# Softmax parts without the row sums: the high part on ScalarE, the sums by transpose and DRAM into the gates

## The chip, the cores and the metric

The kernel runs on one core of a Trainium2 chip. TensorE (PE) multiplies matrices and writes into PSUM, VectorE (DVE), ScalarE (ACT) and GpSimd (POOL) work elementwise, and SyncE (SP) issues the DMAs. Each engine runs its own instructions in order and waits for others by semaphores. The metric is the device time of one execution in microseconds (us).

## The reference

One layer over 1024 frames of 1024 features: a LayerNorm, one wide projection, two attention mixers side by side, and a LayerNorm after the sum. Cut to what matters:

```
proj = h @ w_in + b_in                       # q, k, v, z of mixer A; latents and z of mixer B; two gates
ya = A(q, k, v)                              # 8 heads of 64; own chunk of 64 and 8 before it, relative bias
yb = B(q, k, v)                              # 8 heads; chunk-causal over all keys before
    s = q . k * scale (+ bias);  p = softmax(s);  y = p @ v
ya = (ya * silu(a_z)) @ w_proj_a
yb = (yb * silu(b_z)) @ w_proj_b
out = (sigmoid(g_a) * ya + sigmoid(g_b) * yb) @ w_out
h = LN(alpha * h + out)
```

## The kernel before

All large products are made of three float32r matmuls of high and low parts (`three`, lines 166 to 169). The work has three stretches: entry, LayerNorm and values (to about 174 us), attention (174 to 746 us), and the projection of mixer B with the output product (to the end). In the attention stretch two streams are woven by `run` (line 270): attention steps and the dense chunks (`Chunk`, line 171), which make q, k, z and the gates for later. The weave goes by estimated costs written in the code.

An attention step is one tile of 128 queries of one head: `scores` (lines 684 and 781) leaves the scores in a PSUM tile `ps` of two banks of 512 columns, and DVE moves them to SBUF with the row's extreme `nm` (lines 697 and 796). `softmax` (line 805) takes exp on ACT with the row sum `su`, turns the sum into a reciprocal and a scaled reciprocal on DVE, lets POOL write the float16 high part `hi` (line 816) and DVE the low part `lo` (line 817), and SP transposes both by DMA into `pT` (line 819). `pv` (line 822) multiplies with the values three tiles later in mixer A and two in mixer B (LAG_A, LAG_B; `Steps.one`, line 847). A tile has 128 to 640 key columns in A and 128 to 1024 in B. Every fourth tile `finish_y` (line 716) takes y from PSUM, and POOL multiplies it with the gate `sz` (line 728), which `evac_silu` (line 708) made from z; `sz` has two buffers, one for each half of 512 frames, and holds two heads in its 128 partitions. The result goes to DRAM (`y_d`) and is read back (`yr`) later, or, for the last heads of B, stays in SBUF as `YB`.

The tile `p16` that holds `hi` and `lo` has three buffers in A and two in B, and the ring `st` of 512 columns has five, shared by gates, y and loads. The order in which instructions stand in each engine's queue is made at build time by a scheduler that works with its own estimate of durations (line 1155); the chip then runs each queue in order. Nearly all DMAs are issued by SP: weights (line 135), transposes, gates and y.

```python
            A.activation(s[:, :n], s[:, :n], AF.Exp, scale=-1.0, bias=nm, accum_out=su)
            V.reciprocal(rc, su)
            V.tensor_scalar(rc2, rc, 2.0 ** 14, None, op0=ALU.mult)
            G.tensor_scalar(hi, s[:, :n], rc, 2.0 ** 14, op0=ALU.mult, op1=ALU.mult)
            V.scalar_tensor_tensor(lo, s[:, :n], rc2, hi, op0=ALU.mult, op1=ALU.subtract)
            SY.dma_start(pT[:, : 2 * n // P, :], p16[:, : 2 * n], transpose=True)
```

Of the kernel before, what the change touches and what calls it, by code (L numbers as in the profile page):

```python
# [18 lines left out]
P = 128  # L19
S = 1024  # L20
# [35 lines left out]
def tile_hybrid_layer(  # L56
# [45 lines left out]
    kr_d = [dram.tile([32, S], F32, name=f"kr_d{i}") for i in range(2)]  # L102
    y_d = [dram.tile([512, S], F32, name=f"y_d{i}") for i in range(2)]
    th_d = [dram.tile([D, S], F32, name=f"th_d{i}") for i in range(2)]


    ident = consts.tile([P, P], F32, name="ident")
# [519 lines left out]
    with ExitStack() as p1:  # L627
# [24 lines left out]
        class PairA:  # L652
# [31 lines left out]
            def scores(self, e, i):  # L684
                h = 2 * self.p + e
                k0 = max(0, i - 4)
                n = (i - k0 + 1) * P
                ps = ps_sc.tile([P, 2, 512], F32, tag="sc", name=f"sa{h}_{i}")
                nb, w = (1, max(n, 256)) if n <= 512 else (2, n // 2)
                for b in range(nb):  # L690
                    ks = slice(k0 * P + b * w, k0 * P + b * w + w)
                    T.matmul(ps[:, b, :w], self.sQ[e][:, i * P : (i + 1) * P], self.sK[e][:, ks], start=True, stop=False)
                    T.matmul(ps[:, b, :w], self.sX[e][:, i * P : (i + 1) * P], self.sK[e][:, ks], start=False, stop=True)
                w = min(w, n)
                s = pools["s"].tile([P, 640], F32, tag="s", name=f"ss{h}_{i}")
                nm = sm.tile([P, 1], F32, tag="nm", name=f"nm{h}_{i}")
                V.tensor_tensor_reduce(  # L697
                    s[:, :n].rearrange("p (b w) -> p b w", b=nb),
                    ps[:, :nb, :w],
                    self.tb[e][:, 640 - n : 640].rearrange("p (b w) -> p b w", b=nb),  # L700
                    -0.125, 3e38, ALU.add, ALU.min, nm,
                )
                return s, nm, n

            def tail(self, e, half, yt, r):
                finish_z(self, 0, e, half, yt, r)
# [27 lines left out]
        class PairB:  # L734
# [46 lines left out]
            def scores(self, e, i):  # L781
                h = 2 * self.p + e
                n = (i + 1) * P
                ps = ps_sc.tile([P, 2, 512], F32, tag="sc", name=f"sb{h}_{i}")
                nb, w = (1, max(n, 256)) if n <= 512 else (2, n // 2)
                qs = slice(i * P, (i + 1) * P)
                for b in range(nb):
                    ks = slice(b * w, b * w + w)
                    T.matmul(ps[:, b, :w], self.sQ[e][:, qs], self.sK[e][:, ks], start=True, stop=False)
                    T.matmul(ps[:, b, :w], self.sX[e][:, qs], self.sK[e][:, ks], start=False, stop=False)  # L790
                    T.matmul(ps[:, b, :w], self.qr[e][:, qs], krt[:, ks], start=False, stop=True)
                w = min(w, n)
                V.memset(ps[0:64, nb - 1, w - 64 : w], NEG)
                s = pools["s"].tile([P, S], F32, tag="s", name=f"sbs{h}_{i}")
                nm = sm.tile([P, 1], F32, tag="nm", name=f"nmb{h}_{i}")
                V.tensor_scalar(  # L796
                    s[:, :n].rearrange("p (b w) -> p b w", b=nb), ps[:, :nb, :w], -B_SCALE, None,
                    op0=ALU.mult, op1=ALU.min, accum_out=nm,
                )
                return s, nm, n  # L800

            def tail(self, e, half, yt, r):
                finish_z(self, 1, e, half, yt, r)

        def softmax(pair, e, i, nm_):
            s, nm, n = pair.scores(e, i)
            su = sm.tile([P, 1], F32, tag="su", name=f"su{nm_}")
            A.activation(s[:, :n], s[:, :n], AF.Exp, scale=-1.0, bias=nm, accum_out=su)  # L808
            rc = sm.tile([P, 1], F32, tag="rc", name=f"rcp{nm_}")
            V.reciprocal(rc, su)  # L810
            rc2 = sm.tile([P, 1], F32, tag="rc2", name=f"rcs{nm_}")
            V.tensor_scalar(rc2, rc, 2.0 ** 14, None, op0=ALU.mult)
            W_ = pools["w"]
            p16 = pools["p"].tile([P, 2 * W_], F16, tag="p16", name=f"p16{nm_}")
            hi, lo = p16[:, :n], p16[:, n : 2 * n]
            G.tensor_scalar(hi, s[:, :n], rc, 2.0 ** 14, op0=ALU.mult, op1=ALU.mult)  # L816
            V.scalar_tensor_tensor(lo, s[:, :n], rc2, hi, op0=ALU.mult, op1=ALU.subtract)  # L817
            pT = pools["pt"].tile([P, 2 * W_ // P, P], F16, tag="pt", name=f"pT{nm_}")
            SY.dma_start(pT[:, : 2 * n // P, :], p16[:, : 2 * n], transpose=True)
            return pT  # L820

        def pv(pair, mixer, e, i, pT, v16):
            h = 2 * pair.p + e
# [15 lines left out]
        class Steps:  # L839
# [7 lines left out]
            def one(self):  # L847
                pair, e, i = self.seq[self.at]
                self.at += 1
                nm = f"{self.m}_{2 * pair.p + e}_{i}"  # L850
                self.q.append((pair, e, i, softmax(pair, e, i, nm)))
                if i == 6:
                    self.next_head()
                if len(self.q) > self.lag:
                    self.fin()
# [5 lines left out]

            def fin(self):
                pair, e, i, pT = self.q.pop(0)
                pv(pair, self.m, e, i, pT, V16[2 * self.m + pair.p // 2])

            def units(self, n):
# [292 lines left out]
```

## Time and profile before

| | |
|---|---|
| time, median of 3 runs | 892.89 us (891.52 to 894.52) |
| the profiled execution | 892.41 us, span 890.6 us |
| instructions | 13773 |
| mean granted TensorE clock | 0.977 |
| DMA | 124.68 MB, mean 140 GB/s |

The span runs from the first to the last instruction. Clock 1 is 2.4 GHz; a mean below 1 says that part of the stretch ran at 1.2 GHz. "A <- B" in a list of waits means that engine and line A sat idle until B was done. Times in a timeline count from the span's start.

### The profile page before, as it was taken

The numbers are of one execution on the slowest core, as the hardware profiler recorded it, in microseconds if no ns is written. First come the engines' busy times: TensorE is split into PE (matmuls) and PEld (weight loads), VectorE is DVE, ScalarE is ACT, GpSimd is POOL, SyncE is SP. The second block draws the span as 40 slices with busy tenths as digits, with TensorE's granted clock in tenths as the row PEclk, the third lists the DMA queues.
The fourth block names the chain that finished last, engine by engine and source line by source line (L and its number), as shares of the span: only waits on it lengthen the run. The fifth ranks groups of instructions, "written<-read, shape, count | busy, mean of one in ns | idle before, by whom it ended". The sixth has DMA issues, their size and how long they took to land. (4 is left out here: it accounts for less than half of the span.)

```text
span 890.6 us, 13773 instructions
## 1 busy us (share of the span) xinstructions
PE 832.0 (93%) x4760; PEld 697.9 (78%) x4760; DVE 570.3 (64%) x1267; ACT 359.0 (40%) x729; POOL 397.3 (45%) x413
## 2 busy tenths in 40 slices
PE   5999899998999896999999999999998899999996
PEld 4999798887777685778787877888777787888886
DVE  6899655577687769756655655265606584657654
ACT  4234475445455535545443444354425251422000
POOL 5547541344554445834333943253445373641100
PEclk8999899999999999899999999999999899999999
DMA  6522013376678564595665567556866879551421
GB/s 204 204 106 80 32 42 101 139 150 134 147 150 173 128 145 115 99 206 115 141 154 148 107 153 149 163 119 133 186 176 134 197 194 288 178 165 60 142 95 47
DMA packets 185365, 124.68 MB, mean 140 GB/s; under 512 B 146160, under 2 KB 149744, under 8 KB 185296
## 3 DMA queue, kind: packets, MB, share of 16 engines
q1 hardware_dynamic: 185296, 123.82, 56.0%
q8 instruction: 37, 0.61, 0.3%
q14 instruction: 32, 0.26, 0.1%
HBM read 57.98 MB, written 22.81 MB: 91 GB/s over the span
## 5 line engine op out<-in xcount | busy, mean ns | idle before, releaser
L167 PE MATMUL dn<-hT,wh_c 128*128 128x512 f32 x512 | 206.6, 404 | 5.4 <-DVE sK L643 2.3
L169 PE MATMUL dn<-hT,wl_c 128*128 128x512 f32 x512 | 203.8, 398 | 0.0
L168 PE MATMUL dn<-hT,wh_c 128*128 128x512 f32 x512 | 203.3, 397 | 0.0
L132 POOL TENSOR_TENSOR wl_c<-wr_c,wh_c 128x512 fp32r<-128x512 f32 x64 | 86.1, 1346 | 117.7 <-ACT wh_c L131 103.2
L167 PEld LDWEIGHTS dn<-hT,wh_c 128*128 128x128 f32 x512 | 97.8, 191 | 24.6 <-DVE bQ L640 2.4
L169 PEld LDWEIGHTS dn<-hT,wl_c 128*128 128x128 f32 x512 | 97.6, 191 | 20.1
L168 PEld LDWEIGHTS dn<-hT,wh_c 128*128 128x128 f32 x512 | 97.9, 191 | 18.1
L817 DVE SCALAR_TENSOR_TENSOR p<-sbs,rcs,p 128x128 f16<-128x128 f32 (+3 forms) x64 | 70.2, 1099 | 24.7 <-POOL p L816 22.9
L816 POOL TENSOR_SCALAR p<-sbs,rcp 128x128 f16<-128x128 f32 (+3 forms) x64 | 49.7, 777 | 75.0 <-DVE rcp L810 57.8
L131 ACT ACTIVATE wh_c<-wr_c 128x512 fp32r<-128x512 f32 x64 | 40.3, 630 | 84.0 <-DMA wr_c<-in_wch_dram 61.2
L817 DVE SCALAR_TENSOR_TENSOR p<-ss,rcs,p 128x640 f16<-128x640 f32 (+2 forms) x64 | 59.2, 936 | 21.0 <-POOL p L816 19.9
L808 ACT ACTIVATE sbs<-sbs,nmb 128x128 f32<-128x128 f32 (+3 forms) x64 | 49.5, 774 | 56.1 <-DVE sbs L796 49.1
L728 POOL TENSOR_TENSOR yt<-yt,sz 64x512 f32<-64x512 f32 x32 | 43.4, 1355 | 52.5 <-DVE yt L722 35.7
L816 POOL TENSOR_SCALAR p<-ss,rcp 128x640 f16<-128x640 f32 (+2 forms) x64 | 45.6, 717 | 41.5 <-DVE rcp L810 27.9
L808 ACT ACTIVATE ss<-ss,nm 128x640 f32<-128x640 f32 (+2 forms) x64 | 44.4, 694 | 46.4 <-DVE nm L697 39.3
L831 PE MATMUL y<-pT,v16b 128*128 128x128 f16 x576 | 45.4, 222 | 8.6 <-DMA pT<-p 8.4
L169 PE MATMUL ops<-wo,mixT 128*128 128x512 f32 (+1 forms) x144 | 53.1, 369 | 0.0
L168 PE MATMUL ops<-wo,mixT 128*128 128x512 f32 (+1 forms) x144 | 52.9, 369 | 0.0
L831 PEld LDWEIGHTS <-v16b 128*128 128x128 f16 x576 | 33.5, 99 | 23.8 <-issue 22.6
L831 PE MATMUL y<-pT,v16a 128*128 128x128 f16 x480 | 38.4, 223 | 14.6 <-DMA pT<-p 13.4
L167 PE MATMUL ops<-wo,mixT 128*128 128x512 f32 (+1 forms) x144 | 51.7, 369 | 0.0
L831 PEld LDWEIGHTS <-v16a 128*128 128x128 f16 x480 | 28.8, 99 | 26.2 <-issue 21.1
(247 smaller groups left out, 1891.2 us busy)
## 6 DMA issues: line engine op xcount, KB each, us to landing
wr_c<-in_wch_dram SPq DMA_DIRECT2D x64, 256.0 KB, 3.1
th_d<-g SPq DMA_DIRECT2D x32, 256.0 KB, 2.5
th<-th_d SPq DMA_DIRECT2D x32, 256.0 KB, 3.3
h_d<-xt SPq DMA_DIRECT2D x8, 512.0 KB, 2.6
sX<-sQ SPq DMA_DIRECT2D x16, 256.0 KB, 4.6
sXb<-bQ SPq DMA_DIRECT2D x16, 256.0 KB, 3.9
r<-h_d SPq DMA_DIRECT2D x8, 512.0 KB, 3.5
wor<-in_wo_dram SPq DMA_DIRECT2D x16, 256.0 KB, 2.9
```

The lines of the kernel that those rows point to most:

```text
L131: A.activation(hi, raw, AF.Copy)
L132: (eng or V).tensor_tensor(lo, raw, f(hi), op=ALU.subtract)
L167: T.matmul(ps, ah, bh, start=start, stop=False)
L168: T.matmul(ps, ah, bl, start=False, stop=False)
L169: T.matmul(ps, al, bh, start=False, stop=stop)
L728: G.tensor_tensor(yt[r, :], yt[r, :], pair.sz[half][r, :], op=ALU.mult)
L808: A.activation(s[:, :n], s[:, :n], AF.Exp, scale=-1.0, bias=nm, accum_out=su)
L816: G.tensor_scalar(hi, s[:, :n], rc, 2.0 ** 14, op0=ALU.mult, op1=ALU.mult)
L817: V.scalar_tensor_tensor(lo, s[:, :n], rc2, hi, op0=ALU.mult, op1=ALU.subtract)
L831: T.matmul(o, v16[:, k0 + k, h % 4, :], pT[:, a * nk + k, :], start=(k == 0 and a == 0), stop=(k == nk - 1 and a == 1))
```

## The change

The softmax step no longer divides by the row sum. ACT writes the high part itself, as exp times 2^14 in float16, and DVE subtracts it from exp times 2^14 for the low part. The row sums of four tiles gather in the four columns of one tile `su`. Two steps after the fourth tile (at tile 1 or 5 of the next group), `norm` transposes this 128x4 tile on TensorE into columns 384 to 511 of the second bank of the current scores' PSUM tile, DVE writes the reciprocal as four rows of 128, SP stores these in DRAM (`rc_d`) and loads them back as one row of 512 broadcast to 64 partitions into a tile of the `st` ring, and POOL multiplies the half's gate `sz` with it. For the last half of a mixer's last head, `norm` runs in `fin` ahead of `pv` with a PSUM tile of its own.

```diff
@@ -102,6 +102,7 @@
     kr_d = [dram.tile([32, S], F32, name=f"kr_d{i}") for i in range(2)]
     y_d = [dram.tile([512, S], F32, name=f"y_d{i}") for i in range(2)]
     th_d = [dram.tile([D, S], F32, name=f"th_d{i}") for i in range(2)]
+    rc_d = [dram.tile([8, S], F32, name=f"rc_d{i}") for i in range(2)]
 
 
     ident = consts.tile([P, P], F32, name="ident")
@@ -700,7 +701,7 @@
                     self.tb[e][:, 640 - n : 640].rearrange("p (b w) -> p b w", b=nb),
                     -0.125, 3e38, ALU.add, ALU.min, nm,
                 )
-                return s, nm, n
+                return s, nm, n, ps
 
             def tail(self, e, half, yt, r):
                 finish_z(self, 0, e, half, yt, r)
@@ -797,27 +798,41 @@
                     s[:, :n].rearrange("p (b w) -> p b w", b=nb), ps[:, :nb, :w], -B_SCALE, None,
                     op0=ALU.mult, op1=ALU.min, accum_out=nm,
                 )
-                return s, nm, n
+                return s, nm, n, ps
 
             def tail(self, e, half, yt, r):
                 finish_z(self, 1, e, half, yt, r)
 
         def softmax(pair, e, i, nm_):
-            s, nm, n = pair.scores(e, i)
-            su = sm.tile([P, 1], F32, tag="su", name=f"su{nm_}")
-            A.activation(s[:, :n], s[:, :n], AF.Exp, scale=-1.0, bias=nm, accum_out=su)
-            rc = sm.tile([P, 1], F32, tag="rc", name=f"rcp{nm_}")
-            V.reciprocal(rc, su)
-            rc2 = sm.tile([P, 1], F32, tag="rc2", name=f"rcs{nm_}")
-            V.tensor_scalar(rc2, rc, 2.0 ** 14, None, op0=ALU.mult)
+
+            s, nm, n, ps = pair.scores(e, i)
+            if i % 4 == 0:
+                sums[pair, e, i // 4] = sm.tile([P, 4], F32, tag="su", name=f"su{nm_}")
+            A.activation(s[:, :n], s[:, :n], AF.Exp, scale=-1.0, bias=nm, accum_out=sums[pair, e, i // 4][:, i % 4 : i % 4 + 1])
             W_ = pools["w"]
             p16 = pools["p"].tile([P, 2 * W_], F16, tag="p16", name=f"p16{nm_}")
             hi, lo = p16[:, :n], p16[:, n : 2 * n]
-            G.tensor_scalar(hi, s[:, :n], rc, 2.0 ** 14, op0=ALU.mult, op1=ALU.mult)
-            V.scalar_tensor_tensor(lo, s[:, :n], rc2, hi, op0=ALU.mult, op1=ALU.subtract)
+            A.activation(hi, s[:, :n], AF.Copy, scale=2.0 ** 14)
+            V.scalar_tensor_tensor(lo, s[:, :n], 2.0 ** 14, hi, op0=ALU.mult, op1=ALU.subtract)
             pT = pools["pt"].tile([P, 2 * W_ // P, P], F16, tag="pt", name=f"pT{nm_}")
             SY.dma_start(pT[:, : 2 * n // P, :], p16[:, : 2 * n], transpose=True)
-            return pT
+            return pT, ps
+
+        sums = {}
+
+        def norm(mixer, pair, e, half, ps):
+
+
+            nm = f"{mixer}_{2 * pair.p + e}_{half}"
+            r = slice(64 * e, 64 * e + 64)
+            T.transpose(ps, sums.pop((pair, e, half)), ident)
+            row = sm.tile([4, P], F32, tag="srow", name=f"srow{nm}", bufs=2)
+            V.reciprocal(row, ps)
+            d = rc_d[mixer][2 * pair.p + e : 2 * pair.p + e + 1, half * 512 : half * 512 + 512]
+            SY.dma_start(d.rearrange("o (a b) -> (o a) b", a=4), row)
+            rb = st.tile([P, 512], F32, tag="st", name=f"rb{nm}")
+            SY.dma_start(rb[r, :], d.broadcast_to([64, 512]))
+            G.tensor_tensor(pair.sz[half][r, :], pair.sz[half][r, :], rb[r, :], op=ALU.mult)
 
         def pv(pair, mixer, e, i, pT, v16):
             h = 2 * pair.p + e
@@ -848,7 +863,11 @@
                 pair, e, i = self.seq[self.at]
                 self.at += 1
                 nm = f"{self.m}_{2 * pair.p + e}_{i}"
-                self.q.append((pair, e, i, softmax(pair, e, i, nm)))
+                pT, ps = softmax(pair, e, i, nm)
+                self.q.append((pair, e, i, pT))
+                if i in (1, 5) and self.at > 2:
+                    past = self.seq[self.at - 3]
+                    norm(self.m, past[0], past[1], past[2] // 4, ps[0:4, 1, 384:512])
                 if i == 6:
                     self.next_head()
                 if len(self.q) > self.lag:
@@ -861,6 +880,9 @@
 
             def fin(self):
                 pair, e, i, pT = self.q.pop(0)
+                if i % 4 == 3 and (pair, e, i // 4) in sums:
+                    ps = ps_sc.tile([P, 2, 512], F32, tag="sc", name=f"sup{self.m}_{2 * pair.p + e}")
+                    norm(self.m, pair, e, i // 4, ps[0:4, 0, 0:P])
                 pv(pair, self.m, e, i, pT, V16[2 * self.m + pair.p // 2])
 
             def units(self, n):
```

## Rows read from the trace of the kernel before

**Rows 1.** The page, part 1: busy us, share of span, instructions of each engine.
```profile
PE 832.0 (93%) x4760; PEld 697.9 (78%) x4760; DVE 570.3 (64%) x1267; ACT 359.0 (40%) x729; POOL 397.3 (45%) x413
```
**Rows 2.** TensorE's waits: total, times, longest us; whole span, last row 640 to 700.
```profile
PE y L831 <- DMA pT<-p: 21.9, 19, 2.6
...
PE dn L167 <- DVE sK L643: 2.3, 2, 1.6
...
PE sa L692 <- DVE nm L697: 0.6, 2, 0.3
...
PE y L831 <- DMA pT<-p: 6.4, 3, 2.6
```
**Rows 3.** Windows: stretch, length, busy us of engines, granted clock, DMA share, GB/s.
```profile
200.00:250.00 50.00, 46.13 (x295) 38.25 (x294) 32.85 (x89) 25.03 (x53) 26.18 (x32) 0.97 0.69 148
...
350.00:400.00 50.00, 44.04 (x267) 35.69 (x268) 33.90 (x74) 25.35 (x54) 32.26 (x35) 0.93 0.72 145
650.00:700.00 50.00, 43.65 (x231) 35.86 (x230) 21.62 (x52) 19.49 (x37) 21.93 (x20) 0.90 0.72 160
```
**Rows 4.** Timeline, 296 to 312 us: start, length, instruction, idle time before it.
```profile
299.28 0.19 ACT L808 ACTIVATION_READ_ACCUMULATOR ss<-ss,nm 128x1 f32 x1
...
300.64 0.79 POOL L816 TENSOR_SCALAR p<-ss,rcp 128x640 f16<-128x640 f32 x1
...
303.27 0.89 DVE L817 SCALAR_TENSOR_TENSOR p<-ss,rcs,p 128x640 f16<-128x640 f32 x1 [0.30 <-DVE rcp L810]
...
304.22 8.47 SPq L819 DMA_TRANSPOSE pT<-p  x4
...
307.64 0.83 PE L831 MATMUL y<-pT,v16a 128*128 128x128 f16 x12 [1.65 <-DMA pT<-p]
```
**Rows 5.** Timeline of ACT, DVE, SP and PE, 660 to 698 us.
```profile
662.06 0.19 ACT L808 ACTIVATION_READ_ACCUMULATOR sbs<-sbs,nmb 128x1 f32 x1
...
663.03 0.35 DVE L817 SCALAR_TENSOR_TENSOR p<-sbs,rcs,p 128x128 f16<-128x128 f32 x1 [0.40 <-POOL p L816]
...
664.54 1.18 SPq L819 DMA_TRANSPOSE pT<-p  x1
...
668.73 0.27 PE L831 MATMUL y<-pT,v16b 128*128 128x128 f16 x2 [2.06 <-DMA pT<-p]
```
**Rows 6.** Groups by line and form: count, busy us, mean ns, idle before.
```profile
L131 ACT ACTIVATE wh_c<-wr_c 128x512 fp32r<-128x512 f32 x64 | 40.3, 630 | 84.0 <-DMA wr_c<-in_wch_dram 61.2 <-PE dn L168 21.1 <-PE sa L693 1.3
...
L810 DVE RECIPROCAL rcp<-su 128x1 f32<-128x1 f32 x128 | 20.3, 160 | 45.1 <-ACT sbs L808 29.3 <-ACT ss L808 14.4
L812 DVE TENSOR_SCALAR rcs<-rcp 128x1 f32<-128x1 f32 x128 | 19.3, 152 | 3.2
...
L349 PE MATMUL hps<-ident,xt 128*128 128x128 f32 x64 | 9.3, 290 | 7.6 <-DVE xt L342 7.6
...
L533 ACT ACTIVATE v16a<-vs_a 128x256 f16<-128x256 f32 x16 | 6.5, 412 | 2.8 <-POOL vs_a L531 2.6
```
**Rows 7.** DMA issues: count, KB each, median us from issue to landing.
```profile
y_d<-yt SPq DMA_DIRECT2D x28, 128.0 KB, 2.5
yr<-y_d SPq DMA_DIRECT2D x14, 256.0 KB, 3.4
```
**Rows 8.** Waits of ACT, then of POOL, whole span.
```profile
ACT wh_c L131 <- DMA wr_c<-in_wch_dram: 61.2, 30, 6.0
...
POOL p L816 <- DMA pT<-p: 13.6, 7, 2.7
```
**Rows 9.** Timelines of POOL, ACT, DVE and PE, around the last gate and YB.
```profile
670.43 1.27 POOL L728 TENSOR_TENSOR yt<-yt,sz 64x512 f32<-64x512 f32 x1
...
681.18 0.68 ACT L712 ACTIVATE sz<-dn,bcol 128x512 f32<-128x512 f32 x1
...
749.52 0.69 DVE L132 TENSOR_TENSOR YB<-yt,YB 64x512 fp32r<-64x512 f32 x1
...
752.46 0.39 PE L167 MATMUL pj<-YB,wh_p 128*128 128x512 f32 x1
```

## The prediction

> **What bounds the kernel now.** I read the page's first part first: TensorE is busy 832.0 of 890.6 us, DVE, ACT and POOL well under two thirds [rows 1]. So the change can win only what TensorE loses, and every TensorE instruction that it adds stands on the path that sets the end. The second view was TensorE's waits. The largest by far is matmul L831 (probabilities times V) waiting for pT: 21.9 us in 19 waits, the longest 2.6; 6.4 us of that, three waits, lie between 640 and 700 us. Next come dense matmuls waiting for a PSUM buffer that DVE has not emptied: 2.3 us behind sK, and the same once more, 1.6 us, behind bQ, of which the first stands [rows 2]. The third view was the windows over the attention stage. In four of 50 us between 200 and 700 the granted clock is clearly below 1: 0.97 twice (one of them shown), 0.93 and 0.90 of 2.4 GHz [rows 3], so part of each runs at the lower level of 1.2 GHz. Matmul time lost is 1.5 + 1.5 + 3.5 + 5.0 = 11.5 us. Before the falls TensorE idled: the three windows shown have 3.9, 6.0 and 6.4 us without matmul. The pT waits with the clock behind them thus cost about 33 us, and this is what the change can reach.
>
> The fourth view, the timeline of two late tiles, shows where lateness comes from. In the first, exp with its row sum is done at 299.47; POOL begins the high part at 300.64, DVE the low part only at 303.27, the DMA transpose is issued at 304.22, and L831 runs at 307.64 after 1.65 us of waiting [rows 4]. So 4.7 us pass between the sum and the end of the low part, of which the two conversions are 0.79 + 0.89; the rest is queueing on two engines and the reciprocal. In the second tile (128 columns) the low part is done at 663.38, but the transpose is issued at 664.54 and TensorE starts at 668.73, after 2.06 us: there the DMA is late, not the arithmetic [rows 5].
>
> **The change part by part.** The sum is made on the profiled execution, 892.41 us, which is 1.8 over its span and 0.5 under the median of 892.89.
>
> *The softmax step, 128 times.* It loses a reciprocal and a scaling on DVE (20.3 + 19.3 = 39.6 us over all) [rows 6]. The high part moves from POOL (0.79 us at 640 columns, rows 4) to ACT. No ACT copy of 640 columns is in the trace, but 0.41 us at 256 and 0.63 at 512 [rows 6] give 0.85 ns a column, so an estimate of 0.74 us at 640. Mean widths are 480 and 576 columns in the two mixers: 64 x (0.60 + 0.68) = 82 us more for ACT, 359 to 441 us, half of the span. As an operation it is a swap of equals; the gain is that the chain exp, reciprocal, POOL, DVE becomes exp, ACT, DVE, with the second ACT instruction directly behind the first. In rows 4 the low part could be done some 0.74 + 0.89 us after 299.47, at 301.1 instead of 304.2: 3 us, more than the 1.65 lost. In rows 5 sum and low part are only 1.13 us apart, of which the change saves a few tenths; the 2.06 us stay.
>
> So I count by place. The three waits after 640 (6.4 us, the only large ones in that stretch) I leave. Of the other 15.5 us I take two thirds, 10.3; the bounds are 0 (each cut only uncovers the DMA, as in rows 5) and all 21.9. The clock behind them: 6.5 us in the three windows before 400, two thirds of that 4.3; the 5.0 after 650 stay; bounds 0 and 11.5. The dense matmuls' waits for DVE (3.9 us): DVE gives back 39.6 of its 570 us, and I take half, 2.0; bounds 0 and 3.9. Gain: 16.6 us.
>
> *The row sums, 32 times* (two mixers, eight heads, two halves). Each is a TensorE transpose of 128x4, a DVE reciprocal from PSUM, a row written to DRAM, the row read back into 64 partitions, and a POOL multiplication of the gate. The TensorE part has no cover. The nearest row is L349, fp32 transposes of 128x128: 64 in 9.3 us busy, 0.145 each, 0.290 from start to end of one [rows 6]. I take 32 x 0.145 = 4.6 us; bounds 0 (all fall into idle time) and 32 x 0.29 = 9.3, since one transpose alone among matmuls may not be pipelined with its neighbours.
>
> The Trainium skill (TensorE: Matmul & The Clock Gate, Part 4: PE-mode transpose) speaks for the dearer side: about 275 ns for one in a kernel's context, most of it the access latency. By it the 32 would take 8.8 us and the forecast would be 4 us longer. The row has that as the length of one, but half of it as the distance between two in a row; a transpose by itself is not in this trace.
>
> Half of the transposes (those at tile 5) write into a PSUM bank that the same step's scores also use, so they wait until DVE has read the scores, and behind them on TensorE's queue stand scores and dense matmuls. The nearest row is a score matmul waiting for that same DVE read: 0.6 us in 2 waits, 0.3 each [rows 2]. I take 8 of the 16 at 0.3, 2.4 us; bounds 0 and 16 x 0.9 = 14, a DVE pass of the size of the low part in rows 4. At tile 1 the second bank is unused.
>
> The DRAM trip is two transfers: y_d, a row write of this kind, lands in 2.5 us, yr, a read back, in 3.4 [rows 7], so about 6 us and 64 more issues on SP. What hides it: only the gate waits for it, by POOL, and behind that POOL multiplication stand the splits of the next weights, which are loaded a chunk ahead. The gates have two buffers. At the last pair the old gate is used for the last time at 670.43 to 671.7, and ACT writes the next one into the freed buffer at 681.18 [rows 9]: 9.5 us, so 6 us and a multiplication still fit. If that cover went, a dense matmul would wait for its PSUM buffer, at three changes of pair. At the end of the attention the second half of YB is ready at 750.21, and projection matmuls first read it in the group that begins at 752.46 [rows 9], after nine of its matmuls (9 x 0.23): about 4.3 us of cover. The last transpose stands in the queue before the last L831, so the trip ends 3 to 5 us later than today's gate. I take 1 us; bounds 0 and 5.
>
> *The fuller queues.* ACT waits in order for weight loads (61.2 us in 30 waits), and it now also waits for a free p16 buffer, where POOL waits 13.6 us in 7 [rows 8]. Behind it stand the PSUM evacuations that dense matmuls wait for. I take 2 us, as much as the sK waits cost now [rows 2]; bounds 0 and 13.6.
>
> Sum: -16.6 + 4.6 + 2.4 + 1 + 2 = -6.6 us, so 885.8 by this execution and 886.3 by the median; I say 886.
>
> **The rivals.**
> 1. *The chain had been everything.* All pT waits, the clock loss and the DVE waits go, and only the transposes are paid: -21.9 - 11.5 - 3.9 + 4.6 = -32.7, so 860. For it: rows 4. Against: rows 5, and TensorE that no longer stalls arrives earlier at the next pT, with a lag still fixed at 3 and 2 tiles.
> 2. *The waits move.* Only a third of waits and clock comes back (8.3 us) for the same 10 us of cost: +1.7, 894.5. For it: in rows 5 transposes set the landing, and these stay.
> 3. *SP's queue turns it round: slower.* The read may be issued only once the write has landed; while SP waits those 2.5 us, a pT transpose behind it waits too. It decides where the scheduler leaves nothing ready to put between write and read, and where the delay exceeds what a tile has in hand; 19 of 128 have nothing in hand now. If 11 of the 32 trips make a tile late by today's mean wait (21.9/19 = 1.15 us) with today's share of clock loss (11.5/19 = 0.6), that is 19 us on top of rival 2: about 913; with half as many, 904. Against: SP's list is scheduled with such landings in mind, and SP is idle for much of the stage.
>
> The Trainium skill (DMA: Bandwidth & Descriptors, Two DMAs through the same engine are not ordered) supports the wait: the issuing engine must wait on the first DMA's semaphore before it issues the dependent one. No trace here shows the pair yet.
>
> 4. *ACT becomes the narrow place: slower.* The 13.6 us of p16 waits fall on ACT, and half reaches TensorE through late evacuations (6.8), while the gain is half (8.3) against the 8 us of the other costs: +6.5, about 899. For it: in rows 8 ACT already idles in order. Against: a chain that is faster frees p16 earlier.
>
> **How the numbers follow.** Forecast (878 to 890) 0.37; rival 1 (under 878) 0.12; rival 2 (890 to 897) 0.20; rival 3 (897 to 913) 0.19; rival 4 (895 to 903) 0.12. The range 867 to 904 leaves out the lower part of rival 1 and the upper of rival 3. Both signs hold much of it; the forecast's own range is 878 to 890. What can be told from no change is about 0.3%, 2.7 us. Faster: forecast and rival 1, 0.49 and 0.01 of rival 2, 0.50. Same: most of rival 2, 0.17. Slower: rivals 3 and 4 and the rest of 2, 0.33.
>
> **What would show it.** In the profile after: L831's waits on pT near 12 us, with their rest after 640; clock near 1 in the windows before 400; the new transposes at about 0.15 us each of TensorE's busy time, with less than 3 us of waits in front; ACT busy near 441 us. Wrong would be: pT waits of 20 us or more (rival 2 or 3, told apart by SP's waits in front of the read), TensorE waits on ACT of several us (rival 4), or transposes of 0.3 us and up, which would take the gain by themselves.

## The result, and the profile after

The changed kernel takes 940.96 us (median of 4, 939.08 to 943.49) against 892.83 for the kernel before on the same chip: 1.054 times, interval 1.0507 to 1.0572. That is 48 us slower, 55 us beyond the forecast of 886 and above the range's upper end of 904. The profiled execution has a span of 938.1 us and a mean granted clock of 0.958.

The page's first part, to be set against [rows 1]:

```profile
PE 846.0 (90%) x4792; PEld 709.3 (76%) x4792; DVE 554.5 (59%) x1043; ACT 430.5 (46%) x857; POOL 350.1 (37%) x317
```

POOL and DVE do less, ACT 71.5 us more, as worked out. TensorE has 32 more instructions and 14 us more of busy time, but the span grew by 47.5: the other 33.5 us, most of the loss, is TensorE standing still. Its waits (engine, line, what it waited for: us in total, times, longest), which answer to [rows 2]:

```profile
PE y L846 <- DMA pT<-p: 34.6, 35, 3.6
PE pj L168 <- DVE ya L249: 5.5, 2, 4.3
PE dn L168 <- ACT g L289: 5.2, 1, 5.2
PE sup L828 <- ACT ss L811: 4.1, 1, 4.1
PE sa L693 <- DVE srow L830: 3.9, 3, 1.4
PE dn L168 <- DVE bK L641: 2.3, 1, 2.3
```

The pT waits were to fall from 21.9 us to about 12; they rose to 34.6, in 35 places where there had been 19. New ones stand behind ACT (5.2 and 4.1 us), behind DVE at ya (5.5) and at the reciprocal (3.9); the dense matmuls' wait for a DVE evacuation, 2.3 us, is as long as before, at another tile. Windows of the attention stage (from:to, length, busy us and count of PE, PEld, DVE, ACT, POOL; clock; DMA share; GB/s) answer to [rows 3]:

```profile
200.00:250.00 50.00, 45.40 (x277) 36.88 (x277) 32.40 (x56) 29.09 (x59) 19.27 (x18) 0.97 0.72 153
350.00:400.00 50.00, 35.89 (x219) 27.87 (x219) 39.12 (x73) 30.92 (x66) 26.79 (x25) 0.83 0.67 126
700.00:750.00 50.00, 38.71 (x226) 31.46 (x224) 27.53 (x52) 22.59 (x44) 18.64 (x13) 0.86 0.65 160
```

TensorE now idles 14.1 us between 350 and 400, where it idled 6.0, and the clock there fell from 0.93 to 0.83; between 700 and 750, where it had idled 0.2 us at full clock, it idles 11.3 at 0.86. The first of the three windows is much as before. The last of them, in the kernel before:

```profile
700.00:750.00 50.00, 49.77 (x296) 40.04 (x295) 32.42 (x70) 18.03 (x34) 28.59 (x24) 1.00 0.81 204
```

POOL and SP show where the lateness starts. POOL's waits, then those of SP's DMA queue, then ACT's largest:

```profile
POOL wl_c L133 <- ACT wh_c L132: 169.8, 36, 11.9
POOL sz L835 <- DMA rb<-rc_d: 137.4, 25, 13.2
```

```profile
SPq L136 <- POOL wl_c L133: 66.2, 28, 11.2
SPq L731 <- POOL yt L729: 35.5, 17, 5.5
SPq L834 <- DMA rc_d<-srow: 16.7, 14, 2.6
```

```profile
ACT wh_c L132 <- DMA wr_c<-in_wch_dram: 72.5, 29, 7.9
```

POOL stands 137 us at the gate multiplication (L835), waiting for the row to come back. SP waits 35.5 us at the head of its queue for a y that POOL has not finished (14.3 before), and 16.7 us between the trip's write (L832) and its read (L834). The largest of SP's rows above, weight loads behind POOL's low parts (66.2), is no sign of the loss by itself: it was 58.8 before. In the kernel before:

```profile
SPq L135 <- POOL wl_c L132: 58.8, 23, 11.2
SPq L730 <- POOL yt L728: 14.3, 14, 2.8
```

One trip in the timeline (start, duration, engine, line, tile; in brackets the idle time before and what ended it) shows how these join. POOL, SP, DVE, ACT and PE in turn:

```profile
299.23 1.50 POOL L835 TENSOR_TENSOR sz<-sz,rb 64x512 f32<-64x512 f32 x1 [9.90 <-DMA rb<-rc_d]
300.81 1.75 POOL L729 TENSOR_TENSOR yt<-yt,sz 64x512 f32<-64x512 f32 x1
302.63 1.29 POOL L133 TENSOR_TENSOR wl_c<-wr_c,wh_c 128x512 fp32r<-128x512 f32 x1
```

```profile
293.10 0.43 SPq L832 DMA_DIRECT2D rc_d<-srow  x1
296.20 0.47 SPq L834 DMA_DIRECT2D rb<-rc_d  x1
296.78 1.25 SPq L818 DMA_TRANSPOSE pT<-p  x1
302.58 0.47 SPq L731 DMA_DIRECT2D y_d<-yt  x1
303.95 0.35 SPq L136 DMA_DIRECT2D wr_c<-in_wch_dram  x1
304.41 3.26 SPq L818 DMA_TRANSPOSE pT<-p  x2
```

```profile
298.75 0.82 DVE L816 SCALAR_TENSOR_TENSOR p<-ss,p 128x640 f16<-128x640 f32 x1 [0.42 <-ACT p L815]
300.33 1.08 DVE L816 SCALAR_TENSOR_TENSOR p<-ss,p 128x640 f16<-128x640 f32 x1 [0.76 <-ACT p L815]
```

```profile
307.23 0.63 ACT L132 ACTIVATE wh_c<-wr_c 128x512 fp32r<-128x512 f32 x1 [5.76 <-DMA wr_c<-in_wch_dram]
307.76 0.81 ACT L811 ACTIVATE ss<-ss,nm 128x640 f32<-128x640 f32 x1
```

```profile
308.50 0.72 PE L846 MATMUL y<-pT,v16a 128*128 128x128 f16 x10 [1.12 <-DMA pT<-p]
```

The write is issued at 293.10 and POOL has the row at 299.23, 6.1 us later, just the 6 us that were estimated (5.6 is the median of the 25 trips for which POOL waited, worked out from the timelines). But POOL has stood since 289.33, and behind the multiplication stand y times gate and a weight's low part. SP's next instruction is the store of that y, issued at 302.58; the weight load behind it starts at 303.95, just after POOL's low part is done (302.63 + 1.29). Only then come the two transposes whose low parts were ready at 299.57 and 301.41. The late load keeps ACT idle for 5.76 us, and the next exp begins at 307.76. So the first transpose is issued 4.8 us after its low part was ready, the second right behind it, and ACT stands 5.8 us; TensorE pays 1.12 us at 308.50. This is one trip; what all of them cost is for the experiments to say.

### The profile page after: what moved, and what is told of

The parts are those of the page before. It is cut to its first block, busy times and chain, and to the rows that moved or that the text cites. A ratio compares the mean times of both kernels' runs of the same rounds, so it can differ in the third digit from the quotient of the medians.

```text
span 938.1 us, 13770 instructions
## 1 busy us (share of the span) xinstructions
PE 846.0 (90%) x4792; PEld 709.3 (76%) x4792; DVE 554.5 (59%) x1043; ACT 430.5 (46%) x857; POOL 350.1 (37%) x317
## 4 chain that ended last, share of the span: by engine, by line
PE 33%; DMA 9%; POOL 3%; DVE 2%; ACT 1%; issue 1%; SPq 1%; DVEq 0%; POOLq 0%; ACTq 0%
PE dn L168 5%; PE dn L170 4%; PE dn L169 4%; PE ops L168 3%; PE ops L170 3%; PE ops L169 3%; DMA pT<-p 2%; PE y L846 2%; PE pj L168 2%; PE pj L169 2%; PE pj L170 2%; DMA wor<-in_wo_dram 1%; DMA wr_c<-in_wch_dram 1%; DMA rb<-rc_d 1%; DMA wr_p<-in_wpb_dram 1%
## 5 line engine op out<-in xcount | busy, mean ns | idle before, releaser
L170 PE MATMUL dn<-hT,wl_c 128*128 128x512 f32 x512 | 205.1, 401 | 1.0 <-POOL wl_c L133 1.0
L169 PE MATMUL dn<-hT,wh_c 128*128 128x512 f32 x512 | 204.2, 399 | 0.0
L170 PEld LDWEIGHTS dn<-hT,wl_c 128*128 128x128 f32 x512 | 98.6, 193 | 21.7 <-POOL wl_c L133 1.4
L169 PEld LDWEIGHTS dn<-hT,wh_c 128*128 128x128 f32 x512 | 98.4, 192 | 18.3 <-issue 0.2
L835 POOL TENSOR_TENSOR sz<-sz,rb 64x512 f32<-64x512 f32 x32 | 44.6, 1394 | 168.9 <-DMA rb<-rc_d 137.4
L816 DVE SCALAR_TENSOR_TENSOR p<-sbs,p 128x128 f16<-128x128 f32 (+3 forms) x64 | 62.0, 972 | 53.7 <-ACT p L815 53.1
L816 DVE SCALAR_TENSOR_TENSOR p<-ss,p 128x640 f16<-128x640 f32 (+2 forms) x64 | 56.5, 888 | 41.5 <-ACT p L815 40.9
L132 ACT ACTIVATE wh_c<-wr_c 128x512 fp32r<-128x512 f32 x64 | 40.2, 628 | 85.3 <-DMA wr_c<-in_wch_dram 72.5
L811 ACT ACTIVATE ss<-ss,nm 128x640 f32<-128x640 f32 (+2 forms) x64 | 44.2, 691 | 35.5 <-DVE nm L698 35.3
L794 DVE MEMSET sb<- 64x64 f32 x64 | 7.1, 112 | 84.6 <-PE sb L792 84.0
L846 PE MATMUL y<-pT,v16a 128*128 128x128 f16 x480 | 40.4, 230 | 15.4 <-DMA pT<-p 15.3
L168 PE MATMUL ops<-wo,mixT 128*128 128x512 f32 (+1 forms) x144 | 51.3, 369 | 2.1 <-ACT wo L132 2.1
L170 PE MATMUL ops<-wo,mixT 128*128 128x512 f32 (+1 forms) x144 | 52.3, 365 | 0.0
L169 PE MATMUL ops<-wo,mixT 128*128 128x512 f32 (+1 forms) x144 | 52.1, 365 | 0.0
L729 POOL TENSOR_TENSOR yt<-yt,sz 64x512 f32<-64x512 f32 x32 | 46.2, 1444 | 15.8 <-DVE yt L723 13.6
L846 PEld LDWEIGHTS <-v16a 128*128 128x128 f16 x480 | 31.3, 103 | 26.9 <-issue 23.4
```

The source lines that it names most:

```text
L132: A.activation(hi, raw, AF.Copy)
L168: T.matmul(ps, ah, bh, start=start, stop=False)
L169: T.matmul(ps, ah, bl, start=False, stop=False)
L170: T.matmul(ps, al, bh, start=False, stop=stop)
L729: G.tensor_tensor(yt[r, :], yt[r, :], pair.sz[half][r, :], op=ALU.mult)
L816: V.scalar_tensor_tensor(lo, s[:, :n], 2.0 ** 14, hi, op0=ALU.mult, op1=ALU.subtract)
```

## The experiments

Three theories. A: POOL stands at the gate multiplication, and what waits for POOL is late. B: SP stands between write and read, and the transposes behind it are late. C: ACT's new work is too much. Each ratio below is to the kernel before on the same chip; differences between kernels measured on different chips are differences of ratios times 893 us, by their intervals good to some 3 to 5 us.

### The softmax step alone

**e1**, the kernel before with the high part on ACT:

```diff
-            G.tensor_scalar(hi, s[:, :n], rc, 2.0 ** 14, op0=ALU.mult, op1=ALU.mult)
+            A.activation(hi, s[:, :n], AF.Copy, scale=rc2)
```

> The first half of the change alone, on the kernel before: the row sums, reciprocals and the normalised parts stay, only the high part moves from POOL to ACT (scaled by rc2). Theory A (the trip of the sums into the gate costs the 48 us, through the POOL gate and the y_d store that stand in front of loads and transposes on SP): this runs without them, so 880 to 893 us, pT waits not above 22 us. Rival C (ACT is the narrow place: p16 waits and evacuations behind the high part): 915 to 940 us, with waits on ACT of 10 us or more at TensorE. Rival D (any rewritten order costs this much): above 900.

Measured: 885.78 us, ratio 0.9898 (0.9852 to 0.9945). The pT waits, before 21.9 in 19:

```profile
PE y L831 <- DMA pT<-p: 15.9, 22, 1.5
```

**e2**, the changed kernel with both calls of `norm` taken out:

```diff
-                    norm(self.m, past[0], past[1], past[2] // 4, ps[0:4, 1, 384:512])
-                    norm(self.m, pair, e, i // 4, ps[0:4, 0, 0:P])
```

> The changed kernel without norm: high part by ACT, sums gathered, but no transpose, reciprocal, DRAM trip or gate multiplication, so the output lacks the division by the row sums. Theory A and rival B (SP waits between write and read): 875 to 890 us, since all that they blame is gone. Rival C (ACT): 915 us or more, since the load of ACT is that of the changed kernel.

Measured: 882.98, ratio 0.988 (0.9834 to 0.9927). In both, ACT carries the high part and the time falls, so C falls. e2 leaves out the division by the sums. The softmax half of the change gains 9 to 11 us; everything lost lies in `norm`.

### A ladder through norm

**e4**, transpose and reciprocal stay, both DMAs and the multiplication go; **e5**, only the multiplication goes:

```diff
# e4
-            SY.dma_start(d.rearrange("o (a b) -> (o a) b", a=4), row)
-            rb = st.tile([P, 512], F32, tag="st", name=f"rb{nm}")
-            SY.dma_start(rb[r, :], d.broadcast_to([64, 512]))
# e4 and e5
-            G.tensor_tensor(pair.sz[half][r, :], pair.sz[half][r, :], rb[r, :], op=ALU.mult)
```

> The changed kernel with transpose and reciprocal, but without the two DMAs and the gate multiplication (the division by the sums is left out of the output). Theory A and rival B: 5 to 12 us above the kernel without norm (transposes 4.6 us, reciprocals of 0.94 us on DVE that score matmuls wait for), so 882 to 900. Rival E (the reciprocal from PSUM, 0.94 us each, 32 times, is what delays DVE and TensorE): 920 or more.

> The changed kernel with transpose, reciprocal and both DMAs of the trip, but without the gate multiplication that waits for them (the division by the sums is left out of the output). Theory A: near the kernel without the trip, at most 8 us above it, since the y_d store no longer waits for the trip: 885 to 905 us. Rival B (SP's own wait between write and read): near the changed kernel, 925 to 941.

Measured: e4 892.54, ratio 0.997 (0.9944 to 0.9996); e5 915.77, ratio 1.0251 (1.0203 to 1.0299). So transposes and reciprocals cost 8.0 us, the two DMAs that nobody reads 25.1, the multiplication that waits for them 25.8: -10.7 + 8.0 + 25.1 + 25.8 = 48.2, the whole (by construction, as each step is measured from the one before). e5 lies between the two ranges that were expected of it, so neither A nor B alone is the cause.

### The wait between write and read (B)

**e8** is e5 with the second transfer reading a tensor that nobody writes; **e17** and **e18** are e5 and e8 with one written cost of the weave changed, since the order of every queue is built anew for each kernel and might itself have made the difference:

```diff
# e8
-            SY.dma_start(rb[r, :], d.broadcast_to([64, 512]))
+            SY.dma_start(rb[r, :], lnp_g[:, 0:512].broadcast_to([64, 512]))
# e17 (on e5), e18 (on e8)
-            return (2 if mixer == 0 else 3) * max(n, 256) / 2400 + 0.112 * n / P
+            return (2 if mixer == 0 else 3) * max(n, 256) / 2400 + 0.16 * n / P
```

> The kernel without the gate multiplication (915.8 us), but the second DMA reads 512 values of another DRAM tensor (the last LayerNorm's gain), which nothing writes, so SP does not wait between the two; the division by the sums is left out of the output. Theory B (SP's wait for the landing of the row, 20.0 us in 17 in that kernel, holds up transposes and loads): 893 to 902 us. Rival F (the two extra issues and the tile of the shared ring cost as much): 910 to 917.

> The kernel of e5 (trip without the multiplication) with one constant of the weave's written costs changed from 0.112 to 0.16, which leaves the work as it is and changes the order in which it stands in all queues. It leaves out the division by the row sums. If an order is worth little, the time lies within 5 us of e5's 916; if it is worth as much as what is claimed for SyncE's wait, it may lie anywhere from 893 to 935.

> The kernel of e8 (the second transfer reads another DRAM tensor and so waits for nothing) with the same constant changed to 0.16, in the same order of work as e17 but for the scheduler's own choices. It leaves out the division by the row sums. If SyncE's wait between write and read costs 23 us whatever the order, e17 minus e18 is 18 to 28 us. If the 23 us came from the order, the difference is under 10.

Measured: e8 892.24, ratio 0.9973 (0.995 to 0.9996); e17 923.53, ratio 1.0287 (1.0238 to 1.0337); e18 900.02, ratio 1.0042 (1.002 to 1.0064). SP's wait for the write in front of the read, in e5 and then in e17 (e8 and e18 have no such row):

```profile
SPq L834 <- DMA rc_d<-srow: 20.0, 17, 2.9
```

```profile
SPq L834 <- DMA rc_d<-srow: 18.2, 19, 2.1
```

The pT waits in e5, and in e8:

```profile
PE y L845 <- DMA pT<-p: 27.8, 29, 3.4
```

```profile
PE y L845 <- DMA pT<-p: 20.6, 19, 4.0
```

Twice the same transfers, the same issues and the same bytes; with the wait 915.8, without it 892.2, and in the other order 923.5 and 900.0. The wait costs 22 to 25 us in either order: that SP's wait is a cause is shown. Transfers and issues by themselves cost nothing (e8 against e4). The one other order is worth 3 to 6 us by the ratios, so differences below that are not read as effects here.

How the wait reaches TensorE is shown only in part. The page's first part of e5, then of e8:

```profile
PE 843.4 (92%) x4792; PEld 705.1 (77%) x4792; DVE 542.9 (59%) x1043; ACT 431.6 (47%) x857; POOL 305.8 (33%) x285
```

```profile
PE 831.1 (93%) x4792; PEld 697.3 (78%) x4792; DVE 542.0 (61%) x1043; ACT 432.6 (49%) x857; POOL 307.7 (35%) x285
```

Of the 23.9 us between their spans (915.0 and 891.1) TensorE stands still for 11.6, of which the pT waits are 7.2, and is busy 12.3 longer with the same instructions. The mean granted clock is 0.971 against 0.979, which makes about 8 of these 12 us by an estimate (0.029 x 915 less 0.021 x 891). Transposes do leave later behind the wait, 0.66 us after the end of the low part against 0.53 (0.76 against 0.55 in e17 and e18; means worked out from the timelines); but in e13 below, where SP waits too, it is 0.52, so they are not the whole way.

### The gate that waits (A)

**e12** is the changed kernel with e8's source, so that the multiplication waits, but only for one transfer; **e13** keeps the real trip and multiplies the gate by itself, so that POOL waits for nothing:

```diff
# e13
-            G.tensor_tensor(pair.sz[half][r, :], pair.sz[half][r, :], rb[r, :], op=ALU.mult)
+            G.tensor_tensor(pair.sz[half][r, :], pair.sz[half][r, :], pair.sz[half][r, :], op=ALU.mult)
```

> The changed kernel, whole, but the second DMA of the trip reads another DRAM tensor (the last LayerNorm's gain) that nothing writes, so that neither SP nor the gate multiplication waits for the row to be written; gates are multiplied by that gain instead of by the reciprocal sums. Theory (it is the waits behind the row's landing that cost, on SP and through the late gate on POOL): 892 to 902. Rival H (the multiplication itself, 32 x 1.39 us of POOL in front of the other gate work, costs): 910 to 920, that is 25 above the 892 without it.

> The changed kernel, whole, with both DMAs of the trip and SP's wait between them, but the gate is multiplied by itself, so the POOL multiplication is there and does not wait for the trip (the division by the sums is left out). Theory G (POOL's wait of 137 us for the trip, in front of weights' low parts and gates, is the other 25 us): 912 to 920, the time without a gate multiplication. Rival H (the multiplication's own time on POOL): 932 to 942.

Measured: e12 900.53, ratio 1.0075 (1.0049 to 1.0101); e13 911.44, ratio 1.0202 (1.0166 to 1.0238). With e8 and e5 this makes a square:

| | POOL doesn't wait | POOL waits for the row |
|---|---|---|
| SP doesn't wait | e8 892.2 | e12 900.5 |
| SP waits | e5 915.8, e13 911.4 | changed kernel 941.0 |

The 32 multiplications cost nothing (e13 against e5). Waiting costs 9 us where the row comes by one transfer and 26 to 30 where it comes by two and SP waits too. POOL's row in e12 has 38% of the 137.4 us:

```profile
POOL sz L835 <- DMA rb<-in_lnp_g_dram: 52.6, 20, 13.4
```

### By which path the late gate reaches TensorE

**e9** lets POOL issue the y stores, so that none stands at SP's head. **e14** multiplies y with the row, behind y times gate, rather than the gate at the time of `norm`. **e16** does both. **e15** is e14 with the read issued just ahead of that multiplication.

```diff
# e9, e16
-                SY.dma_start(y_d[mixer][h * 64 : h * 64 + 64, sl], yt[r, :])
+                G.dma_start(y_d[mixer][h * 64 : h * 64 + 64, sl], yt[r, :])
# e14, e16: in norm, then in finish_z
-            G.tensor_tensor(pair.sz[half][r, :], pair.sz[half][r, :], rb[r, :], op=ALU.mult)
+            rbs[mixer, pair.p, e, half] = rb
...
             G.tensor_tensor(yt[r, :], yt[r, :], pair.sz[half][r, :], op=ALU.mult)
+            G.tensor_tensor(yt[r, :], yt[r, :], rbs.pop((mixer, pair.p, e, half))[r, :], op=ALU.mult)
# e15: in finish_z
             G.tensor_tensor(yt[r, :], yt[r, :], pair.sz[half][r, :], op=ALU.mult)
+            rb = st.tile([P, 512], F32, tag="st", name=f"rb{mixer}_{h}_{half}")
+            SY.dma_start(rb[r, :], rbs.pop((mixer, pair.p, e, half)).broadcast_to([64, 512]))
+            G.tensor_tensor(yt[r, :], yt[r, :], rb[r, :], op=ALU.mult)
```

> The changed kernel with the 28 y_d stores issued by POOL, behind the gate multiplication that they wait for, and no longer in SP's queue. Theory A (a y_d store that waits for the trip stands in front of loads and transposes on SP: 35.5 us of such waits against 14.3 before): 941 falls to 912 to 922, the time without the gate multiplication. Rival G (POOL's own wait for the trip delays the low parts of the weights behind it, whoever issues the store): 932 to 945.

> The changed kernel with the POOL multiplication by the reciprocals moved: no longer on the gate at norm time, but on y itself, directly behind y times gate (finish_z), one or more tiles later in POOL's queue. Both transfers and SP's wait between them stay; the result is the reference's. Theory 1 (the price of the waiting multiplication is that POOL's queue stands while the trip is under way, and with it everything that POOL issues behind it): with the wait at the place where the row is needed, POOL's wait for the row falls from 137 us to under 60, and the time falls to 914 to 926, near the 911 to 916 that the kernel takes without POOL's wait. Theory 2 (the price is that y itself, its store and the buffers are late by the trip, wherever POOL waits): POOL's wait may move, but the time stays at 934 to 944. Between 926 and 934 both would have a part.

> The kernel of e14 (multiplication by the reciprocals behind y times gate) with the y stores issued by GpSimd, so that no store of y stands at the head of SyncE's queue. The result is the reference's. In e14 those stores are ahead of 12 late transposes and account for 16 us of their lateness. Theory 1 (SyncE's queue held by stores that wait for y is what is left of the price): 914 to 922. Theory 2 (the rest sits elsewhere, in SyncE's wait for the write and in ring buffers): 926 to 934, as in the pair of e9 and the changed kernel, where the same move gave 4 us.

> The changed kernel with the reciprocals' read from DRAM moved from norm to finish_z, between y times gate and y times reciprocals: write and read then stand one to four DMAs apart in SyncE's queue in mixer A, and the row's ring buffer is held only while it is needed. The result is the reference's. Theory 1 (SyncE's wait between write and read, with the ring buffer held through it, is what is left of the price): SyncE's wait for the write falls under 6 us and the time falls to 905 to 920. Theory 2 (y itself is late by the trip, and what waits for y on SyncE's and GpSimd's queues is the price): the read now lies wholly in y's own path, GpSimd waits for it again (over 60 us), and the time stays at 930 or rises to 945.

Measured: e9 936.84, ratio 1.0468 (1.0429 to 1.0506); e14 932.16, 1.0419 (1.0381 to 1.0457); e16 923.76, 1.0303 (1.0271 to 1.0334); e15 929.77, 1.0364 (1.0325 to 1.0403). POOL's wait for the row in e14, SP's waits in e14, then both in e15:

```profile
POOL yt L732 <- DMA rb<-rc_d: 12.3, 7, 4.1
```

```profile
SPq L734 <- POOL yt L732: 15.4, 11, 5.7
SPq L837 <- DMA rc_d<-srow: 15.3, 16, 1.7
```

```profile
POOL yt L734 <- DMA rb<-rc_d: 80.3, 24, 8.3
```

```profile
SPq L736 <- POOL yt L734: 43.8, 20, 3.9
SPq L733 <- DMA rc_d<-srow: 19.0, 12, 3.2
```

Theory A in its narrow form (the y store is what holds SP) falls with e9: that move alone brings 6 us, little more than an order is worth. Moving POOL's wait alone (e14) brings 11 us, though the wait all but goes. Both together (e16) bring 21, and e16 then lies 1 to 9 us above e17, e5 and e13, where nothing waits for the row. So POOL's lateness costs by more than one way. One is the stores of y at SP's head, for which SP waits 35.5 us in the changed kernel against 14.3 before: taking them off SP brings 6 us alone and 10 on top of e14, though SP's waits for them are only 15.4 there. The rest is not shown. Weight loads that wait for POOL's low parts, as at 303.95 above, hold the transposes in that timeline, but over the whole kernel they wait no longer than elsewhere: 66.2 us in the changed kernel, and more in e2, which takes 883:

```profile
SPq L136 <- POOL wl_c L133: 75.5, 35, 12.1
```

Nor was the ring `st` tested by itself, whose buffers e14 and e16 hold longer. By their numbers e14 lies between its two theories, e16 within 2 us of the first one's bounds, and e15 fits the second: POOL waits 80 us again, and the time is 930. That the two moves of e16 take away all of the price is likely and not shown, as orders differ.

In e15 the read was to stand one to four DMAs behind its write in mixer A; in the timeline it is none to nine there, and none to three in mixer B. Of the 12 reads that waited, ten stood directly behind their write and two had one DMA between; none of the 13 with two or more between waited. In e5, 11 of the 17 stood directly behind it, five had one between and one had two. So in these two kernels three DMAs between write and read covered the landing, and SP stands where the queue has next to nothing to put there.

### Two other repairs, and the version that stays

**e6** takes the reciprocal of 128x4 ahead of the transpose and only copies out of PSUM after it; **e10** lets POOL issue both DMAs of the trip:

```diff
# e6
+            V.reciprocal(rc, su)
-            T.transpose(ps, sums.pop((pair, e, half)), ident)
+            T.transpose(ps, rc, ident)
-            V.reciprocal(row, ps)
+            V.tensor_copy(row, ps)
# e10
-            SY.dma_start(d.rearrange("o (a b) -> (o a) b", a=4), row)
+            G.dma_start(d.rearrange("o (a b) -> (o a) b", a=4), row)
-            SY.dma_start(rb[r, :], d.broadcast_to([64, 512]))
+            G.dma_start(rb[r, :], d.broadcast_to([64, 512]))
```

> The changed kernel with the reciprocal taken on the 128x4 sums before the transpose, and a plain copy of the 4x128 result from PSUM after it. The reciprocal of 4x128 takes 0.94 us in the changed kernel, 32 times; one of 128x1 took 0.16. Theory: the step without the trip cost 9.6 us over no norm at all, of which the long reciprocal is the larger part, so 930 to 937 here against 941. Rival: the transposes and their waits make the 9.6, and this stays within 938 to 944.

> The changed kernel with both DMAs of the trip issued by POOL, so that SP waits for neither the reciprocal nor the row's landing. Theory B: 941 falls by the 23 us that the trip cost on SP, to 915 to 925, if POOL's own waits cost no more than now. Rival G (POOL, which now waits for the landing in front of its other work, becomes the narrow place): 935 to 960.

Measured: e6 935.76, ratio 1.0469 (1.0418 to 1.0519), 6 us under the changed kernel with touching intervals: undecided. e10 951.21, ratio 1.0624 (1.0589 to 1.0659), slower still. POOL now waits at three places of the trip:

```profile
POOL sz L835 <- DMA rb<-rc_d: 66.7, 22, 5.8
POOL rc_d L832 <- DVE srow L830: 58.7, 18, 11.8
POOL rb L834 <- DMA rc_d<-srow: 49.4, 23, 4.1
```

SP's own wait between write and read is gone there, but POOL stands 175 us in place of 137, and SP still waits 37.4 us for a late y. The wait has to leave every queue on which others depend, not only SP's.

**e11** keeps the division in the softmax step, has ACT write the high part, and drops the second scaling:

```diff
-            rc2 = sm.tile([P, 1], F32, tag="rc2", name=f"rcs{nm_}")
-            V.tensor_scalar(rc2, rc, 2.0 ** 14, None, op0=ALU.mult)
-            G.tensor_scalar(hi, s[:, :n], rc, 2.0 ** 14, op0=ALU.mult, op1=ALU.mult)
-            V.scalar_tensor_tensor(lo, s[:, :n], rc2, hi, op0=ALU.mult, op1=ALU.subtract)
+            A.activation(hi, s[:, :n], AF.Copy, scale=rc)
+            V.scalar_tensor_tensor(lo, s[:, :n], rc, hi, op0=ALU.mult, op1=ALU.subtract)
```

(`us`, with which y is scaled, takes 2^-16 in place of 2^-30.)

> Towards a kernel that beats both: the kernel before with the high part on ACT and with the parts of the probabilities unscaled, so that the scaling of the reciprocal on DVE goes (128 of 0.15 us, 19 us of DVE); the factor 2^14 moves into the values' scale. Theory (the chain to pT is what TensorE waits for, and a shorter one gains): 878 to 885, against 885.8 with the scaling. Rival (what the chain still loses lies in the DMA): within 3 us of 885.8.

Measured: 884.89 us, ratio 0.9894 (0.986 to 0.9928): 1.1% under the kernel before, with an interval that leaves out no change, and level with e1. The ranges of its theory and of its rival both hold this, so what dropping the second scaling is worth stays undecided. It has nearly all of what e2 gains, without a trip.

## Why the prediction was wrong

| step | predicted, us | measured, us |
|---|---|---|
| softmax step, with fuller queues | -16.6 + 2 = -14.6 | -10.7 (e2), -9.1 (e1) |
| transposes, bank waits, reciprocals | 4.6 + 2.4 + 0 = 7.0 | 8.0 (e4 against e2) |
| write and read on SP's queue | 0 | 25.1 (e5 against e4) |
| multiplication that waits, end of the attention | 1 | 25.8 (changed against e5) |
| sum | -6.6 | 48.2 |

**The step that failed** is the DRAM trip: "only the gate waits for it, by POOL", and behind that multiplication only splits "which are loaded a chunk ahead". Its duration was right (6.1 us against 6). What was wrong is that a cover was counted by who needs the result, in time until the gate's buffer is needed, and not by who stands behind the waiting instruction. Two queues that run in order wait for the trip: POOL at the multiplication, and SP at the read and again at the stores of a y that POOL has not finished. The waits on SP cost 22 to 25 us (e5 and e8, e17 and e18), POOL's wait another 26 to 30 (the changed kernel against e5 and e13). For the weights, too, the chunk ahead was no cover at 303.95 above: SP's load waits for POOL's low part to free the buffer, the transposes stand behind that load, and ACT waits 5.76 us for it. How much of the whole loss takes this way is open.

**The softmax step** was right in mechanism and 3.9 us too large by e2, 5.5 by e1, little more than the intervals allow. The chain did become shorter: from the end of the row sum to the end of the low part, means over the 64 tiles of each mixer worked out from the timelines, 3.56 and 3.22 us before, 2.38 and 2.53 in e2. In the changed kernel it is still shorter (3.03 and 2.48), but from there to the issue of the transpose it takes 1.16 and 0.79 us where it took 0.40 and 0.30. ACT's new copies are 0.74 us at 640 columns, as estimated, and ACT's busy time is 430.5 against 441.

**The transposes and the reciprocal.** 

```profile
L830 DVE RECIPROCAL srow<-sa x15: 935/942/946, 190.1 to 385.9; 4x128 f32<-4x128 f32 x15
```

```profile
L828 PE MATMUL sa<-ident,su x15: 269/271/415, 186.9 to 381.7; 128*4 128x128 f32 x15
```

(Least, median and greatest duration in ns, first and last start.) The Trainium skill (TensorE: Matmul & The Clock Gate, Part 4: PE-mode transpose) has about 275 ns for one transpose of 128x128 in bf16 in a kernel, and here 0.271 from start to end of one with 4 columns agrees. On TensorE's path a transpose takes less than from its start to its end. One among dense matmuls, in e4:

```profile
201.73 0.39 PE L169 MATMUL dn<-hT,wh_c 128*128 128x512 f32 x1
201.96 0.27 PE L828 MATMUL sa<-ident,su 128*4 128x128 f32 x1
201.99 0.48 PE L170 MATMUL dn<-hT,wl_c 128*128 128x512 f32 x1
202.30 0.40 PE L693 MATMUL sa<-sK,sQ 128*128 128x512 f32 x1
```

Matmuls of this size start 0.23 us apart; the two steps from L169 by L170 to L693 take 0.57 in place of 0.46. So one transpose takes 0.11 us of the path, and 32 about 3.5 us by this estimate: the forecast's 4.6 was the right side, the dearer 8.8 and 9.3 were not.

The reciprocal had been given no price: 0.94 us for 4x128, 30 us of DVE over all. The bank waits were priced at the transposes, behind DVE's reading of the scores, at 2.4 us; there they are 0.3 us, in one wait. In their place score matmuls wait 3.9 us for the reciprocal (L693 behind L830 above), which holds the bank. So the two terms come out near their sum (8.0 against 7.0) partly by luck.

**The rivals.** Rival 3 (SP's queue turns it round, 0.19) had the direction and SP's wait as the cause: 19 us for eleven late tiles, against the 22 to 25 that e8 and e18 show for that wait, with ten and nine more waits for pT (29 against 19 in e5 and e8, 31 against 22 in e17 and e18). The rule it leaned on (the Trainium skill, DMA: Bandwidth & Descriptors, Two DMAs through the same engine are not ordered) agrees with the traces: in e5, e17 and the changed kernel 14 to 19 of the 32 reads wait for their write. Against it had been said that SP's list is scheduled with such landings in mind; in e5 it has nothing between write and read in 11 of the 32 trips, and one DMA in 14. What no rival had is the price of POOL's wait, the other half of the loss. SP's wait alone already leaves the range: 915.8 in e5 and 911.4 in e13, against 904. Rival 4 (ACT) falls with e1 and e2. Its sign came, TensorE's waits of 5.2 and 4.1 us for ACT, but in e2, where ACT has the same copies, the longest is 1.3. ACT's wait for weights (72.5 us for wh_c against 61.2 in [rows 8]) tells nothing: it is no shorter in e11, which takes 884.9:

```profile
ACT wh_c L131 <- DMA wr_c<-in_wch_dram: 76.7, 32, 8.1
```

**The clock** went with the idling, as argued, but the other way: mean 0.958 against 0.977 before, 0.979 in e8 and 0.988 in e11.

## What to carry to other kernels

A wait is priced by what stands behind the waiting instruction on its queue and by the queues that wait for those in turn, not by when its own result is needed: here the waits for a 6 us trip, taken 32 times, cost 50 us though its result had time. Before a DRAM round trip goes onto an in-order queue that also feeds TensorE, test it in two steps: the same DMAs with no dependence between them (free here), and the same work without the consumer's wait. Where a change joins a gain with a new mechanism, try the gain by itself: e11 and e1 keep 9 us of it with a few lines.

## What was not expected of the hardware

The VectorE reciprocal over 512 sums laid out as 4 rows of 128 takes 0.94 us; in e6, where the same sums lie as 128 rows of 4, it takes 0.18. The rows of 128 are read from PSUM, but that is not the price, since e6's plain copy of 4x128 out of PSUM takes 0.27. A long row on few partitions is the dear layout for it:

```profile
L830 DVE RECIPROCAL rc<-su x32: 157/178/180, 180.8 to 783.6; 128x4 f32<-128x4 f32 x32
```

The 32 pairs of transfers on one queue cost 22 to 25 us when the second reads what the first wrote, and nothing (e8 against e4, 0.3 us) when it doesn't.
